# Layer norm two blocks later, a halved merge, another bank for the sigmoid, halved copies, and expert 30 scattered in two float32r parts

## The chip, the cores and the metric

One Trainium2 chip, one core. The metric is the device time of one execution of the whole program in microseconds (us), from the first instruction to the last; the figure that stands for a kernel is the median of its runs.

## The reference, cut to what matters

A decoder block over 256 tokens of 1024 channels, all in float32. In front, an adaLN-modulated RMS norm gives h, and `p = h @ w_in` gives 8 sections of 1024 columns, of which two feed a convolution branch, four an HGRN2 recurrence, and two are gates:

```python
u = conv(a * sigmoid(b), dw) + dw_bias            # 31 taps along the sequence
y_conv = silu(layernorm(u, ln_g, ln_b)) @ w_conv_out
y_hg = hgrn2(q, f, i, g) @ w_hgrn_out
merged = sigmoid(gc) * y_conv + sigmoid(gh) * y_hg
x = x + ga1 * (merged @ w_out)
```

Behind it stands a mixture of 32 experts of which each token takes four. Per expert, with xb its tokens:

```python
u = xb @ w1[e] + b1[e]                             # 1024 -> 2048
gl, lin = minimum(u[:, :1024], 7), clip(u[:, 1024:], -7, 7)
y = (gl * sigmoid(1.702 * gl) * (lin + 1)) @ w2[e] + b2[e]
out[tokens] += y * weight
```

The block ends in a final RMS norm of `x + ga2 * out`.

## The kernel before, in words

**Front.** The weights of the dense products come in 44 blocks of 1 MB (32 of w_in, then four each of ho, co and wo: the two branch outputs and w_out). Each block is split into float32r parts, high and low, in two halves (`split_half`, L381 to L401): ScalarE casts the high part (L393), VectorE or GpSimd subtracts it to get the low part (L395). `SPLIT_DVE` and `SPLIT_HALF` name the blocks whose subtraction VectorE does. A block's product is 48 matmuls of 256 columns on TensorE (L409, three per pair of parts). The halves of block n + 1 are split in program order within the product of block n.

After each block of w_in the kernel steps lists of jobs by one piece: `norms` (the recurrence's output, L592 on), `mods` (adaLN sections, L343), `lns` (the layer norm of the convolution, `layer_norm`, L553 on) and `taps` (the convolution's 31 taps on VectorE, L460). At block `LN_FROM` = 23 all taps that are left are emitted, and then the layer norm is appended; its five pieces run after blocks 23 to 27. The first piece sums `cv`, the convolution's output, over channels on TensorE (`mup`, L255), so it needs the last tap. The second gives the mean (`mu`, L264 and L563). The third subtracts it on VectorE (L565), squares on ScalarE (L569) and sums on TensorE (`varp`, L571). The fourth takes the root (L229, L230) and scales (L579). The fifth is 16 ScalarE activations and four multiplications (L586 to L589). The result is read when it is split for the co products (L416).

**Merge.** After each of the four co blocks, `tm = ps * gate + gate` (L807, L808) is split into float32r parts: `hi` by a ScalarE copy (L810), `lo` by VectorE (L811). `mg[0]` holds blocks 0 and 1, `mg[1]` blocks 2 and 3. The wo products read channel tiles kt 0 to 3 from `mg[0]` and 4 to 7 from `mg[1]`, so kt 6 and 7 are block 3's two halves.

**Experts.** The loop runs over experts 0 to 31; the order of TensorE and of SP's DMA queue is written by hand, while the order of the other engines is set by the framework's scheduler up to the last expert's second layer, from where ScalarE and VectorE are by hand too. Weights come in tiles of 1 MB through 22 slots: eight of w1 and four of w2 per expert. A slot's next load is issued when the products that read it are done. `first_layer` (L1007) fills two PSUM banks, `up[0]` (u_gl) and `up[1]` (u_lin), 64 token rows twice, and then: `gl = min(up[0])` (L1026), sigmoid on ScalarE into `si`, which lies in `up[0]` (L1027), the clip of `up[1]` (L1028), and two more VectorE operations (L1029, L1030). `turn` transposes the result on TensorE into a bank `ta` (L1043), ScalarE copies it (L1045), and `second_layer` reads it (L1058). An odd expert also gathers the tokens of the next pair (`xg_ps`, L983) and turns the pair's one-hot round (`rows_back`, L996 on); gather and transposes stand between the two layers.

The second layer's result is scaled (L1068), and a pair is scattered into four accumulator banks `acc` during the next even expert (`scatter`, L1079). For the pairs up to 28 and 29 the one-hot is unweighted (a comparison with zero, L1002, in float32r) and the weight `by` (L1004) goes into two float32r parts of the result (L1071, L1072). For the last pair (`last`, set when expert 29 makes it) `rows_back` returns a weighted float32 one-hot and no `by`, and expert 30 is scattered alone, in float32, in two parts: one inside expert 31's first layer at kt 4, one after it. At the same kt 4 ScalarE copies `owtx` (L1290) and `ga2x` (L1292), which the last expert's end uses (L1360, L1364). The last expert works in halves (`pieces` = 2), and its second layer, L1377, ends with the residual, the norm and the stores.

An expert with more than 64 tokens runs a branch for the rest (`small_first`, `small_second`, L1091 to L1171). `out_of` empties a PSUM bank in two halves, one on ScalarE (L1110) and one on VectorE (L1111).

Of the kernel before, what the change touches and what calls it, by code (L numbers as in the profile page):

```python
# [17 lines left out]
P = 128  # L18
# [24 lines left out]
TAPS = (1, 0, 0, 0, 5, 4, 10, 6, 5, 5, 13, 6, 16, 14, 17, 11, 5, 8, 0, 6, 0, 0, 0, 0, 0, 3, 13, 9, 17, 15, 9, 5)  # L43
LN_FROM = 23
SPLIT_DVE = (3, 4, 6, 28, 29, 30, 31, 37, 38, 40, 42)
# [45 lines left out]
def block_kernel(ctx, tc, xT_d, x_d, prm_d, con_d, wada0_d, wada_d, bada_d, gfin_d, win_d, wco_d, who_d, wo_d,  # L91
# [620 lines left out]
    for n, b in enumerate(IN_ORDER):  # L712
# [57 lines left out]
        if n in MOD_AT:  # L770
            step(mods, 1)
        elif n > MOD_AT[0]:
            step(mods, MOD_EXTRA.get(n, 0))
        if n == LN_FROM:
            step(taps, 1000)
            lns.append(layer_norm())
# [23 lines left out]
    for b in range(4):  # L800
        ps = block_product(36 + b, yx, "co_ps", last=b == 3)
        if b == 2:
            split_half(40, 0)
        if b % 2 == 0:
            mg.append(split_slot(f"mg{b // 2}"))
        tm = temp("tm").rearrange("p (m t) -> p m t", m=2)
        nc.vector.tensor_tensor(out=tm, in0=ps, in1=gate(b, 0), op=ALU.mult)  # L807
        nc.vector.tensor_tensor(out=tm, in0=tm, in1=gate(b, 1), op=ALU.add)  # L808
        hi, lo = (mg[b // 2][:, j, b % 2 * 2:b % 2 * 2 + 2, :] for j in range(2))
        nc.scalar.copy(out=hi, in_=tm)  # L810
        nc.vector.tensor_tensor(out=lo, in0=tm, in1=hi.bitcast(F32), op=ALU.subtract)  # L811
        if b % 2 == 1:
            free()
        step(preps, 2)
# [176 lines left out]
    def rows_back(o, last=False):  # L991


        wt_ps = bank("wt_ps")[:, 0:T]
        for t in range(NT):
            nc.tensor.transpose(wt_ps[:, t * P:(t + 1) * P], o[:, 1, t, :], ident)  # L996
        if last:
            owt = back()
            nc.scalar.copy(out=owt, in_=wt_ps)
            return owt, None  # L1000
        owt = back(dt=F32R)
        nc.vector.tensor_scalar(out=owt, in0=wt_ps, scalar1=0.0, scalar2=None, op0=ALU.not_equal)  # L1002
        by = med.tile([P, 1], F32, tag="by", bufs=2, name="by")
        nc.vector.tensor_reduce(out=by, in_=wt_ps, axis=mybir.AxisListType.X, op=ALU.add)  # L1004
        return owt, by

    def first_layer(xg, i, w1s, hot, pieces=1):  # L1007
# [14 lines left out]
        li = temp("li")  # L1022
        si = up[0]
        for c in range(0, 512, 512 // pieces):
            c = slice(c, c + 512 // pieces)
            nc.vector.tensor_scalar(out=gl[:, c], in0=up[0][:, c], scalar1=LIMIT, scalar2=None, op0=ALU.min)  # L1026
            nc.scalar.activation(si[:, c], gl[:, c], AF.Sigmoid, scale=ALPHA)  # L1027
            nc.vector.tensor_scalar(out=li[:, c], in0=up[1][:, c], scalar1=LIMIT, scalar2=-LIMIT, op0=ALU.min, op1=ALU.max)  # L1028
            nc.vector.scalar_tensor_tensor(out=li[:, c], in0=li[:, c], scalar=1.0, in1=gl[:, c], op0=ALU.add, op1=ALU.mult)  # L1029
            nc.vector.tensor_tensor(out=li[:, c], in0=li[:, c], in1=si[:, c], op=ALU.mult)  # L1030
# [7 lines left out]
    def turn(li, at_, pieces=1, piece=0):  # L1038
        ta = bank("ta")
        n = 4 // pieces  # L1040
        for j in range(piece * n, (piece + 1) * n):
            c = pick_columns(li, j) if pieces == 1 else li[:, j * P:(j + 1) * P]
            nc.tensor.transpose(ta[:, j * P:(j + 1) * P], c, ident)  # L1043
        c = slice(piece * n * P, (piece + 1) * n * P)
        nc.scalar.copy(out=at_[:, c], in_=ta[:, c])  # L1045

# [44 lines left out]
    def small_first(o, places, weights, hot, w1s, at_, owt, a, b, ps, u):  # L1091
# [20 lines left out]

        out_of(ps)
        for t in range(NT):
# [154 lines left out]
    for e in range(E_RUN):  # L1269
# [4 lines left out]
        if e == E_RUN - 1:  # L1274
            gfin = fetch(("gfin",))
            nc.gpsimd.partition_broadcast(gfin[:, 1, :], gfin[0:1, 0, :])  # L1276
            gfin = [gfin[:, 1, g * 512:(g + 1) * 512] for g in range(2)]
            owtx = back()
            ga2x = [temp("ga2x") for _ in range(2)]
        if i == 1 and e + 1 < E_RUN:  # L1280
# [4 lines left out]
        def w1s(kt):  # L1285
            if e == E_RUN - 1 and kt == 4:

                scatter(*before, slice(0, CAP), ts=(0,))
                for h in range(2):
                    nc.scalar.copy(out=owtx[h * 64:(h + 1) * 64, :], in_=owt[64:128, :])  # L1290
                    for g in range(2):
                        nc.scalar.copy(out=ga2x[g][h * 64:(h + 1) * 64, :], in_=ga2[g * 64:(g + 1) * 64, :])  # L1292
            if inline and kt == KT // 2:
# [8 lines left out]
        if i == 0 and e > 0:  # L1302
            scatter(*before, slice(0, 2 * CAP))
            owt, by = nxt
        if inline:
# [6 lines left out]
        if e == 0:  # L1312
            start_acc(1)
            gather(o, xg, 1)
            owt, by = rows_back(o)
        if i == 1 and e + 1 < E_RUN:
# [12 lines left out]
        if inline:  # L1329
            skip_ahead(f"second{e}" if e != RELOAD_AFTER else "reload")  # L1330
        if e == E_RUN - 1:
            break
        yp = second_layer(at_, lambda k2: keep(w2h, ("w2", e, k2)) if inline else take(("w2", e, k2)), hot)
# [149 lines left out]
```

## Time and profile before

| | us |
|---|---|
| runs | 1322.40, 1324.36, 1326.33 |
| median | 1324.36 |
| the profiled execution's own time | 1321.67 |
| its span, first to last instruction | 1319.9 |
| TensorE busy in the span | 1219.9 (92%) |
| VectorE, ScalarE, GpSimd busy | 545.2, 286.5, 163.4 |
| read from HBM | 477.11 MB, 362 GB/s over the span |

A difference between two kernels is read against the median; the profiled execution is 2.69 us shorter than that, and its span leaves out 1.77 us around it. In the page's strips of 40 slices one slice is 33 us: the front ends in the twelfth, and the experts take the rest. TensorE's busy time counts matmuls whose ends are modelled, so where the weights stream at the DMA's full rate a busy TensorE need not be the bound.

### The profile page before, as it was taken

How to read it: one execution, taken by the hardware profiler on the slowest of the kernel's cores; microseconds unless marked ns; L12 is line 12 of the kernel's file. 1: busy time of each engine (PE TensorE's matmuls, PEld its weight loads, DVE VectorE, ACT ScalarE, POOL GpSimd, SP SyncE). 2: the span in 40 equal slices, each digit the busy share in tenths (PEclk: the TensorE clock that was granted, in tenths of full speed). 3: DMA queues.
4: the chain of work that ended last, by engine and by line, in shares of the span. 5: the costliest groups of instructions: out<-in, count | busy, mean ns of one | idle time of the engine just before them, and what ended most of it. 6: DMA issues, size and time to landing. Idle time of an engine off the chain costs nothing. (4 is left out here: it accounts for less than half of the span.)

```text
span 1319.9 us, 19185 instructions
## 1 busy us (share of the span) xinstructions
PE 1219.9 (92%) x7829; PEld 669.9 (51%) x7829; DVE 545.2 (41%) x1121; ACT 286.5 (22%) x449; POOL 163.4 (12%) x78
## 2 busy tenths in 40 slices
PE   7999998999899999999999889988888898999997
PEld 6899788779864343443434333332323243434432
DVE  4498996545644242332323223232222232323322
ACT  4445444664720010001000000100000000100112
POOL 3258665222300000000000000000000000000000
PEclk9999989999999999999999899999999998999999
DMA  9993335656689999999999999999999999999995
GB/s 381 410 406 130 130 129 198 235 205 236 255 324 410 421 410 419 420 420 419 421 420 421 421 419 421 420 420 420 421 420 418 420 421 419 421 403 420 420 419 202
DMA packets 71399, 480.02 MB, mean 364 GB/s; under 512 B 7521, under 2 KB 8801, under 8 KB 15970
## 3 DMA queue, kind: packets, MB, share of 16 engines
q1 hardware_dynamic: 70834, 477.47, 88.5%
q8 instruction: 91, 1.49, 0.5%
q10 hardware_dynamic: 432, 0.72, 0.2%
q14 instruction: 42, 0.34, 0.1%
HBM read 477.11 MB, written 1.05 MB: 362 GB/s over the span
## 5 line engine op out<-in xcount | busy, mean ns | idle before, releaser
L1019 PE MATMUL u_gl<-w_w,xg 128*64 128x512 f32 x1024 | 270.1, 599 | 23.6 <-DMA w_w<-in_w_dram 23.6
L1019 PE MATMUL u_lin<-w_w,xg 128*64 128x512 f32 x1024 | 266.8, 592 | 0.0
L1058 PE MATMUL yp<-w_w,li 128*64 128x512 f32 x992 | 227.2, 606 | 19.1 <-ACT li L1045 10.5
L1019 PEld LDWEIGHTS u_gl<-w_w,xg 128*64 128x64 f32 x1024 | 75.9, 137 | 165.1 <-issue 88.8
L1026 DVE TENSOR_SCALAR gl<-u_gl 128x512 f32<-128x512 f32 (+1 forms) x33 | 22.3, 675 | 329.1 <-PE u_gl L1019 321.2
L1019 PEld LDWEIGHTS u_lin<-w_w,xg 128*64 128x64 f32 x1024 | 80.6, 137 | 140.0 <-issue 139.9
L1058 PEld LDWEIGHTS yp<-w_w,li 128*64 128x64 f32 x992 | 71.7, 139 | 156.5 <-issue 133.9
L409 PEld LDWEIGHTS p_ps<-h,ws 128*128 128x128 f32 x1152 | 141.4, 194 | 12.1 <-issue 5.9
L409 PE MATMUL p_ps<-h,ws 128*128 128x256 f32 x1152 | 146.2, 287 | 0.0
L1068 DVE TENSOR_TENSOR yg<-yp,ga 64x512 f32<-64x512 f32 x60 | 41.3, 689 | 225.6 <-PE yp L1058 225.0
L395 POOL TENSOR_TENSOR ws<-w_in,ws 128x1024 fp32r<-128x1024 f32 x45 | 113.1, 2527 | 87.2 <-ACT ws L393 77.8
L1276 POOL PARTITION_BROADCAST w_gfin<-w_gfin x1 | 1.3, 1305 | 898.6 <-DMA w_w<-in_w_dram 898.6
L1027 ACT ACTIVATE u_gl<-gl 128x512 f32<-128x512 f32 (+1 forms) x33 | 19.4, 589 | 427.2 <-DVE gl L1026 427.2
L460 DVE SCALAR_TENSOR_TENSOR cv<-u,pre,cv 128x229 f32<-128x229 f32 (+28 forms) x240 | 95.2, 456 | 8.6 <-ACT cv L457 7.9
L983 PE MATMUL xg_ps<-o,w_x 128*128 128x128 f32 (+1 forms) x544 | 65.4, 278 | 13.5 <-DVE li L1028 10.3
L1071 ACT ACTIVATE ys0h<-yg,by 64x512 fp32r<-64x512 f32 x30 | 21.6, 720 | 254.0 <-DVE yg L1068 254.0
L393 ACT CAST ws<-w_in 128x1024 fp32r<-128x1024 f32 x64 | 65.7, 1047 | 46.7 <-PE p_ps L409 17.6
L983 PEld LDWEIGHTS xg_ps<-o,w_x 128*128 128x128 f32 x544 | 62.2, 192 | 26.6 <-DVE li L1028 21.7
L987 DVE TENSOR_SCALAR xg<-xg_ps,g,sh 128x128 f32<-128x128 f32 (+1 forms) x136 | 45.3, 396 | 16.5 <-PE xg_ps L983 11.6
L1045 ACT COPY li<-ta 128x512 f32<-128x512 f32 (+1 forms) x33 | 18.9, 573 | 114.6 <-PE ta L1043 109.2
L395 DVE TENSOR_TENSOR ws<-w_in,ws 128x1024 fp32r<-128x1024 f32 x19 | 27.1, 1439 | 11.2 <-ACT ws L393 11.2
L409 PE MATMUL wo_ps<-ws,mg 128*128 128x256 f32 x192 | 26.0, 295 | 2.7 <-DVE mg L811 2.0
(292 smaller groups left out, 1158.1 us busy)
## 6 DMA issues: line engine op xcount, KB each, us to landing
w_w<-in_w_dram SPq DMA_DIRECT2D x380, 1024.0 KB, 19.9
w_in<-in_win_dram SPq DMA_DIRECT2D x32, 1024.0 KB, 11.0
w_ada<-in_wada_dram SPq DMA_DIRECT2D x24, 1024.0 KB, 16.3
w_ho<-in_who_dram SPq DMA_DIRECT2D x4, 1024.0 KB, 8.2
w_co<-in_wco_dram SPq DMA_DIRECT2D x4, 1024.0 KB, 8.4
w_wo<-in_wo_dram SPq DMA_DIRECT2D x4, 1024.0 KB, 9.6
w_w<-in_w_dram SPq DMA_DIRECT2D x8, 512.0 KB, 15.2
xT<-in_xT_dram SPq DMA_DIRECT2D x1, 1024.0 KB, 6.9
```

The source lines that it names most:

```text
L393: nc.scalar.copy(out=to[:, 0], in_=w[:, ks, :])
L395: (nc.vector if dve else nc.gpsimd).tensor_tensor(out=to[:, 1], in0=w[:, ks, :], in1=to[:, 0].bitcast(F32), op=ALU.subtract)
L409: nc.tensor.matmul(out, lhsT=lt, rhs=rh, start=first and kt == 0 and i == 0, stop=kt == KT - 1 and i == 2, skip_group_check=not first)
L460: nc.vector.scalar_tensor_tensor(out=cv[:, ct, s:], in0=u[i][:, m, :T - s], scalar=tap, in1=cv[:, ct, s:], op0=ALU.mult, op1=ALU.add)
L983: nc.tensor.matmul(ps[:, i, cs], lhsT=x2[:, t, kt * P:(kt + 1) * P], rhs=o[:, 0, t, cs], start=t == 0, stop=t == NT - 1)
L987: nc.vector.tensor_scalar(out=xg[h][:, i, cs], in0=ps[:, i, cs], scalar1=g2[:, kt:kt + 1], scalar2=sh2[:, kt:kt + 1], op0=ALU.mult, op1=AL ...
L1019: nc.tensor.matmul(up[nb][g * 64:(g + 1) * 64, :], lhsT=xg[kt // 4][:, kt % 4, i * CAP:(i + 1) * CAP], rhs=w[:, c:c + 512], start=False, s ...
L1026: nc.vector.tensor_scalar(out=gl[:, c], in0=up[0][:, c], scalar1=LIMIT, scalar2=None, op0=ALU.min)
L1027: nc.scalar.activation(si[:, c], gl[:, c], AF.Sigmoid, scale=ALPHA)
L1058: nc.tensor.matmul(yp[g * 64:(g + 1) * 64, :], lhsT=aT[:, kt % 4, kt // 4, :], rhs=w[:, kk, g * 512:(g + 1) * 512], start=False, stop=kt = ...
L1068: nc.vector.tensor_tensor(out=y[rows, :], in0=yp[gs, :], in1=ga2[gs, :], op=ALU.mult)
L1071: nc.scalar.activation(hi[rows, :], y[rows, :], AF.Copy, scale=by[rows, :])
```

## The change

Six edits. The layer norm is appended at block 25, while the taps are still emitted at block 23. Block 3's merge is done in two halves, with `hi` copied by VectorE. The sigmoid goes to `up[1]`, and the clip is issued ahead of it. `turn` copies two transposes at a time. The overflow branch empties its first bank in one ScalarE copy. The last pair gets the unweighted one-hot and `by` as the pairs ahead of it do, with the weighted one kept as `own` for `owtx`; `ga2x` is made after expert 31's first `turn`.

```diff
-LN_FROM = 23
+TAPS_END = 23
+LN_FROM = 25
...
+        if n == TAPS_END:
+            step(taps, 1000)
         if n == LN_FROM:
-            step(taps, 1000)
             lns.append(layer_norm())
...
-        nc.vector.tensor_tensor(out=tm, in0=ps, in1=gate(b, 0), op=ALU.mult)
-        nc.vector.tensor_tensor(out=tm, in0=tm, in1=gate(b, 1), op=ALU.add)
         hi, lo = (mg[b // 2][:, j, b % 2 * 2:b % 2 * 2 + 2, :] for j in range(2))
-        nc.scalar.copy(out=hi, in_=tm)
-        nc.vector.tensor_tensor(out=lo, in0=tm, in1=hi.bitcast(F32), op=ALU.subtract)
+        for m in (slice(0, 1), slice(1, 2)) if b == 3 else (slice(0, 2),):
+            nc.vector.tensor_tensor(out=tm[:, m], in0=ps[:, m], in1=gate(b, 0)[:, m], op=ALU.mult)
+            nc.vector.tensor_tensor(out=tm[:, m], in0=tm[:, m], in1=gate(b, 1)[:, m], op=ALU.add)
+            if b == 3:
+                nc.vector.tensor_copy(hi[:, m], tm[:, m])
+            else:
+                nc.scalar.copy(out=hi[:, m], in_=tm[:, m])
+            nc.vector.tensor_tensor(out=lo[:, m], in0=tm[:, m], in1=hi[:, m].bitcast(F32), op=ALU.subtract)
...
+        own = None
         if last:
-            owt = back()
-            nc.scalar.copy(out=owt, in_=wt_ps)
-            return owt, None
+            own = back("own")
+            nc.scalar.copy(out=own, in_=wt_ps)
         owt = back(dt=F32R)
...
-        return owt, by
+        return owt, by, own
...
-        si = up[0]
+        si = up[1]
...
+            nc.vector.tensor_scalar(out=li[:, c], in0=up[1][:, c], ..., op0=ALU.min, op1=ALU.max)
             nc.scalar.activation(si[:, c], gl[:, c], AF.Sigmoid, scale=ALPHA)
-            nc.vector.tensor_scalar(out=li[:, c], in0=up[1][:, c], ..., op0=ALU.min, op1=ALU.max)
...
-        c = slice(piece * n * P, (piece + 1) * n * P)
-        nc.scalar.copy(out=at_[:, c], in_=ta[:, c])
+        for j in range(piece * n, (piece + 1) * n, 2):
+            c = slice(j * P, (j + 2) * P)
+            nc.scalar.copy(out=at_[:, c], in_=ta[:, c])
...
-        out_of(ps)
+        nc.scalar.copy(out=a, in_=ps)
...
             owtx = back()
-            ga2x = [temp("ga2x") for _ in range(2)]
...
-                    nc.scalar.copy(out=owtx[h * 64:(h + 1) * 64, :], in_=owt[64:128, :])
-                    for g in range(2):
-                        nc.scalar.copy(out=ga2x[g][h * 64:(h + 1) * 64, :], in_=ga2[g * 64:(g + 1) * 64, :])
+                    nc.scalar.copy(out=owtx[h * 64:(h + 1) * 64, :], in_=own[64:128, :])
...
         if e == E_RUN - 1:
+            ga2x = [temp("ga2x") for _ in range(2)]
+            for g in range(2):
+                for h in range(2):
+                    nc.scalar.copy(out=ga2x[g][h * 64:(h + 1) * 64, :], in_=ga2[g * 64:(g + 1) * 64, :])
             break
```

## Rows read from the trace of the kernel before

**Rows 1.** The page's strip of DMA rates in 40 slices of 33 us, GB/s.

```profile
GB/s 381 410 406 130 130 129 198 235 205 236 255 324 410 421 410 419 420 420 419 421 420 421 421 419 421 420 420 420 421 420 418 420 421 419 421 403 420 420 419 202
```

**Rows 2.** The view of windows at the start of the experts: the stretch, its length, busy us of TensorE, its weight loads, VectorE, ScalarE and GpSimd with their counts, then TensorE's granted clock, the DMA's busy share and GB/s.

```profile
382.00:388.00 6.00, 6.00 (x41) 3.44 (x42) 2.63 (x11) 0.00 (x0) 0.00 (x0) 1.00 0.53 190
```

**Rows 3.** The view of waits, 900 to 1000 us (the middle of the experts): the engine and line that waited and for whom, us in total, times, the longest.

```profile
PE u_gl L1019 <- DMA w_w<-in_w_dram: 9.7, 17, 0.9
```

**Rows 4.** The timeline of TensorE, 1070 to 1135 us (experts 24 and 25): start in us, us, engine, line, operation, out<-in and count, and in brackets the idle time of the engine before it with its releaser.

```profile
1089.07 1.07 PE L1058 MATMUL yp<-w_w,li 128*64 128x512 f32 x2 [0.34 <-ACT li L1045]
1093.72 9.36 PE L1058 MATMUL yp<-w_w,li 128*64 128x512 f32 x30 [3.58 <-issue]
...
1120.04 1.10 PE L1120 MATMUL arm_ps<-arm 128*128 128x64 f32 x8 [1.24 <-DVE arm L1111]
```

**Rows 5.** The view of waits, 1130 to 1283 us (from expert 25's overflow branch to the start of expert 31), columns as in rows 3.

```profile
PE yp L1058 <- ACT li L1045: 2.0, 6, 0.3
...
PE xg_ps L983 <- DVE li L1028: 1.6, 2, 0.8
```

**Rows 6.** The view of windows at the end, columns as in rows 2.

```profile
1290.00:1300.00 10.00, 10.00 (x39) 3.26 (x39) 1.61 (x4) 0.39 (x1) 0.00 (x0) 1.00 0.92 348
1300.00:1305.00 5.00, 4.41 (x18) 1.29 (x18) 1.60 (x4) 1.61 (x4) 0.00 (x0) 1.00 0.46 176
```

**Rows 7.** The timeline of all engines, 1288 to 1320 us (expert 31 and the end), columns as in rows 4.

```profile
1289.72 1.98 PE L1079 MATMUL acc<-ys,owt 64*128 64x512 f32 x4
...
1300.08 0.42 DVE L1030 TENSOR_TENSOR li<-li,u_gl 128x256 f32<-128x256 f32 x1
...
1300.89 0.44 PE L1043 MATMUL ta<-con,li 128*128 128x128 f32 x2
...
1304.13 0.37 ACT L1045 COPY li<-ta 128x256 f32<-128x256 f32 x1 [2.39 <-PE ta L1043]
...
1304.56 5.37 PE L1377 MATMUL yp<-w_w,li 128*64 128x512 f32 x24
```

**Rows 8.** The timeline of TensorE, 195 to 345 us, columns as in rows 4.

```profile
220.75 0.64 PE L255 MATMUL mup<-cv,pre 128*32 128x256 f32 x2 [3.65 <-DVE cv L460]
221.32 7.46 PE L409 MATMUL p_ps<-h,ws 128*128 128x256 f32 x48
...
230.17 6.10 PE L409 MATMUL p_ps<-h,ws 128*128 128x256 f32 x48
```

**Rows 9.** The view of windows behind that stall, columns as in rows 2.

```profile
221.00:223.00 2.00, 2.00 (x10) 1.69 (x9) 0.35 (x1) 0.37 (x1) 0.00 (x0) 0.55 0.93 389
```

**Rows 10.** The timeline of all engines, 225 to 300 us (the layer norm and the blocks beside it), columns as in rows 4.

```profile
239.16 2.19 ACT L569 ACTIVATE csq<-cv 128x512 f32<-128x512 f32 x4
...
239.85 2.09 PE L571 MATMUL varp<-csq,pre 128*32 128x256 f32 x12 [0.44 <-ACT csq L569]
...
251.07 1.28 ACT L229 ACT_TABLE_LOAD   x1
...
262.15 1.09 ACT L586 ACTIVATE sigy<-cv,pre 128x256 f32<-128x256 f32 x2
...
269.05 1.08 ACT L587 ACTIVATE cv<-cv,pre 128x256 f32<-128x256 f32 x2
...
273.65 1.05 ACT L393 CAST ws<-w_in 128x1024 fp32r<-128x1024 f32 x1 [0.56 <-PE p_ps L409]
```

**Rows 11.** The timeline of all engines, 282 to 380 us, around the last merge, columns as in rows 4.

```profile
343.58 4.48 PE L409 MATMUL wo_ps<-ws,mg 128*128 128x256 f32 x36
...
345.15 0.68 DVE L807 TENSOR_TENSOR tm<-co_ps,gates 128x512 f32<-128x512 f32 x1
...
347.18 1.05 ACT L393 CAST ws<-w_wo 128x1024 fp32r<-128x1024 f32 x1
...
348.31 5.14 POOL L395 TENSOR_TENSOR ws<-w_wo,ws 128x1024 fp32r<-128x1024 f32 x2 [9.94 <-ACT ws L393]
...
348.78 2.43 DVE L811 TENSOR_TENSOR mg<-tm,mg 128x512 fp32r<-128x512 f32 x1 [2.21 <-ACT mg L810]
...
348.80 0.50 PE L409 MATMUL wo_ps<-ws,mg 128*128 128x256 f32 x2 [0.74 <-ACT mg L810]
...
351.26 8.56 PE L409 MATMUL wo_ps<-ws,mg 128*128 128x256 f32 x58 [1.96 <-DVE mg L811]
353.80 0.42 DVE L845 TENSOR_TENSOR tmo<-wo_ps,ga 128x256 f32<-128x256 f32 x1 [2.59 <-PE wo_ps L409]
```

**Rows 12.** The view of windows behind that wait, columns as in rows 2.

```profile
351.30:353.00 1.70, 1.70 (x8) 1.70 (x9) 0.00 (x0) 0.00 (x0) 1.70 (x1) 0.50 1.04 439
```

**Rows 13.** The timeline of all engines, 1240 to 1285 us (experts 29 and 30), columns as in rows 4.

```profile
1244.45 3.84 PE L983 MATMUL xg_ps<-o,w_x 128*128 128x128 f32 x32 [0.78 <-DVE li L1028]
...
1249.02 0.59 ACT L1045 COPY li<-ta 128x512 f32<-128x512 f32 x1
...
1249.66 7.09 PE L1058 MATMUL yp<-w_w,li 128*64 128x512 f32 x32 [0.34 <-ACT li L1045]
...
1271.19 0.50 PE L1079 MATMUL acc<-ys0h,owt 128*128 128x512 f32 x1
...
1273.66 0.72 PE L1043 MATMUL ta<-con,li 128*128 128x128 f32 x4 [0.33 <-DVEq L1308]
...
1275.03 2.50 ACT L1292 COPY ga2x<-ga 64x512 f32<-64x512 f32 x4
```

More of the change, by code (lines that the diff above doesn't have):

```diff
@@ L1026, in first_layer @@
             nc.vector.tensor_scalar(out=gl[:, c], in0=up[0][:, c], scalar1=LIMIT, scalar2=None, op0=ALU.min)
+            nc.vector.tensor_scalar(out=li[:, c], in0=up[1][:, c], scalar1=LIMIT, scalar2=-LIMIT, op0=ALU.min, op1=ALU.max)
             nc.scalar.activation(si[:, c], gl[:, c], AF.Sigmoid, scale=ALPHA)
-            nc.vector.tensor_scalar(out=li[:, c], in0=up[1][:, c], scalar1=LIMIT, scalar2=-LIMIT, op0=ALU.min, op1=ALU.max)
             nc.vector.scalar_tensor_tensor(out=li[:, c], in0=li[:, c], scalar=1.0, in1=gl[:, c], op0=ALU.add, op1=ALU.mult)
@@ L1303, in block_kernel @@
             scatter(*before, slice(0, 2 * CAP))
-            owt, by = nxt
+            owt, by, own = nxt
         if inline:
@@ L1314, in block_kernel @@
             gather(o, xg, 1)
-            owt, by = rows_back(o)
+            owt, by, own = rows_back(o)
         if i == 1 and e + 1 < E_RUN:
```

## The prediction, made blind

> **What bounds the kernel now.** I read the strips first, then the waits by stretch, then the timeline where a wait is long. The experts stream weights at 418 to 421 GB/s in 24 of the last 28 slices, while the front runs the DMA at about half of that [rows 1]. So the front is set by compute and the experts mostly by the stream. The stream starts when the front ends: from 382 to 388 us the DMA still idles half the time, because slots come free only as expert 0's products go through TensorE [rows 2]. What the front saves therefore moves the whole stream, one for one.
>
> The stream does not set the end, however. Between 900 and 1000 us TensorE waits for weights 17 times [rows 3]. At 1090 us expert 24 loses time on "issue", expert 25 runs the overflow branch [rows 4], and from then to expert 31 the waits of the matmuls are for other engines [rows 5]. The last weights land at about 1302.3 us (1300 plus 0.46 of 5 us [rows 6]), but TensorE is busy with the second layer until 1309.9 [rows 7]. TensorE is thus late by about 7 us, and its savings from expert 25 on count too. Between the two, a saving on TensorE only lengthens a wait for weights.
>
> How late it is bounds the last gain. Expert 31's w2 is 4 MB, 10 us at 420 GB/s, so its last w1 tile lands at about 1292.3. TensorE reads that tile at about 1297.0, 1.7 us (one tile's eight records) ahead of the second scatter, which ends at 1300.6 and takes 1.9 [rows 7]. This leaves 4.7 us to gain up to there.
>
> **1. The layer norm two blocks later.** The first sum over `cv` waits 3.65 us for the last taps with all of TensorE behind it, and the 48 matmuls behind it take 7.46 us where the next block's 48 take 6.10 [rows 8]. In that stretch the granted clock is 0.55, near the lower of the two levels, 1.2 GHz, where it had been 2.4 [rows 9]. The taps are still emitted at block 23. At block 25, two products of 6.1 us later, they are long done, so both losses go: 3.65 + 1.36 = 5.0 us. What is late next? Blocks 24 and 25 were split before the stall, so their products can follow at once. But ScalarE now has the norm's work in blocks 27 to 29, with the recurrence's output beside it and the casts of later blocks (the two of block 30 end at 274.7, behind the sigmoids, and wait for a slot [rows 10]). Now the squares make TensorE wait 0.44 us [rows 10]. There is no row for the new neighbours: the loss lies between nothing and the sigmoid piece, 262.15 to 270.1 or 8.0 us [rows 10]. I take 1.0, near the row of the present wait, since the casts can still be ordered ahead of a piece that nothing needs for several blocks. Net 4.0 us (-3.0 to 5.0).
>
> **2. The halved merge.** Now the wo product runs 36 matmuls to 348.06, then waits 0.74 us for ScalarE's `hi` and 1.96 for `lo`; the 58 matmuls behind take 8.56 us where 58/48 of 6.10 are 7.37, at a granted clock of 0.50 [rows 8, 11, 12]. That is 2.70 + 1.19 = 3.9 us. After the change block 3 takes eight VectorE operations of 128x256, 0.42 us each by the nearest row [rows 11]. The copy's own price shows nowhere; I use the same 0.42, which is what two-operand work of that size costs, and zero to 0.68 bounds it. Started at 345.15, the first half (kt 6) is ready at 346.8 and the second at 348.5; TensorE wants kt 6 at about 348.0 and kt 7 six matmuls, 0.75 us, later [rows 11]. The stall goes. Next in line is block 41, whose low parts GpSimd makes from 348.31 to 353.45 [rows 11]: its first half is ready at about 350.9, and TensorE would arrive at 349.6. I charge 0.9 of this. Net 3.0 us (0 to 3.9).
>
> VectorE's `lo` took 2.43 us against 0.68 for the multiplication of the same size at 345.15, while GpSimd worked [rows 11]. The Trainium skill, page "SBUF — State Buffer", section "Who interferes with whom", says that a VectorE operation with two SBUF inputs, or a copy in a two-port mode, and a GpSimd operation shut each other out for a whole instruction. By that rule this edit, which turns two operations of the kind (the addition and the subtraction) into six, could lose its gain; that case is rival B, and its price follows from the rows.
>
> **3. Experts 25 to 30.** With the sigmoid in `up[1]`, the first bank is free after the minimum, before TensorE is done with the second. The gather of an odd expert, which waits 0.78 us for the clip, need not [rows 5, 13]: 2 x 0.78 = 1.6 (experts 27 and 29; in 25 the branch stands between). The sigmoid now waits for the clip, 0.7 us more of delay; the gather of 3.84 us covers it in odd experts [rows 13], the scatter (1271.19 to 1273.33, eight records) nearly in even ones [rows 13]: at worst 0.2 each. The halved copy costs ScalarE 2 x 0.37 instead of 0.59 [rows 7, 13], but its first half ends before the bias matmuls do, so TensorE's 0.34 us per expert goes: six times, 2.0 [rows 5]. The single copy in the branch (0.59 on ScalarE) replaces a sequence that ended with VectorE's half, at a wait of 1.24 [rows 4]: 0.2. Sum 3.8 us (2.5 to 4.0). The same edits in earlier experts are hidden by the stream.
>
> **4. The end.** Each of the two float32 scatters takes four records, 1.91 us; the pairs' float32r ones take eight in 2.14 (1271.19 to 1273.33), so four take about 1.0 [rows 7, 13]. That gives 1.8 us, on TensorE's own path. Expert 30's two products gain ScalarE and VectorE work (0.7 us operations, half a dozen) that starts seven us ahead of the first scatter: free. What is late next is `li`: its first half ends at 1300.50, and the transposes start at 1300.9 [rows 7]. With the scatter 0.9 shorter they wait up to 0.5. Then `ga2x`: four copies, 2.50 us [rows 13], now stand in a gap of ScalarE of 2.39 [rows 7], ahead of the second `turn`'s copy, unless the scheduler puts some earlier. I charge 0.4 (0 to 1.2). Net 0.9 us (0 to 1.8).
>
> **Sum.** 4.0 + 3.0 + 3.8 + 0.9 = 11.7 us. Up to the last w1 tile parts 3 and half of 4 make 4.7, as much as the weights allow. Against the profiled execution's 1321.67 this gives 1310.0; that execution is 2.69 faster than the median of 1324.36, and against the median the forecast is **1312.7 us**.
>
> **Rivals.**
>
> A. *The norm's stall only moves.* ScalarE is in order; the squares or the casts then make TensorE wait about 4 us in blocks 27 to 31. For it: the casts already stand behind the sigmoids. Against it: two blocks of slack are left. 1312.7 + 4.0 = 1316.7.
>
> B. *GpSimd shuts VectorE out of the merge.* Two operations blocked at 2.43 - 0.68 = 1.75 each are 3.5 us, more than part 2. Against it: GpSimd starts at 348.31, when the chain is nearly done [rows 11]. 1315.7.
>
> C. *Expert 24's loss on "issue" goes or another comes.* It costs 3.58 us and then 9.36 - 7.09 x 30/32 = 2.7 at a slow clock, 6.3 in all [rows 4, 13], just ahead of the stretch where TensorE sets the end. Code of another length can shift such a wait: 1306.4 without it, 1319.0 with a second one behind it.
>
> D. *The front's gain stops at the stream.* Then only parts 3 and 4 are left, 1324.36 - 4.7 = 1319.7. Against it: the idle DMA of [rows 2].
>
> E. *Slower: the norm bunches up on ScalarE.* Squares 2.2, sigmoids 8.0 and two table loads of 1.28 [rows 10] in front of the casts of blocks 30 and 31 give 12.8 us, GpSimd's subtraction behind the cast 2.6 [rows 11], two slow stretches of 1.36: 18.1. Above 12.7 us of such waits (5.0 + 3.0 + 3.8 + 0.9) it is slower than before: 1324.36 + 18.1 - 12.7 = 1329.8. Against it: in the kernel before the same pieces beside the same products left TensorE waiting 0.44 us.
>
> F. *An edit does not do what it says*, as when the scheduler orders VectorE so that the merge's halves come out one behind the other: about 1315.7 too.
>
> **How the numbers follow.** Forecast 0.40, A 0.13, B 0.14, C faster 0.10 and slower 0.07, D 0.08, E 0.05, F 0.03. The range reaches from C's gain together with the upper bounds of the parts (5.0 + 3.9 + 4.0 + 1.8 = 14.7, or 1309.7 without C) up past D: 1304.5 to 1321. It leaves out E and the far ends. A measurement of this kernel tells about 0.3%, 4.0 us, from no change; so faster means below 1320.4. All cases but part of D and of C's slower side, and E, lie there: faster 0.84, the same 0.11, slower 0.05.
>
> **What would show it.** In the profile after: no wait of `mup` for the taps and no granted clock near 0.55 behind it; the wo product without waits for `mg`, or with one for GpSimd; the first expert's products some 7 us earlier; no 0.34 us ahead of the second layers and no 0.78 ahead of gathers; float32r scatters of 1.0 us in expert 31. The forecast is wrong if TensorE waits for ScalarE's casts in blocks 27 to 31, if the stream starts no earlier, or if TensorE waits for weights in expert 31.

## The result, and the profile after

The changed kernel took **1315.67 us** (median of 8 runs, 1313.03 to 1321.19), the kernel before 1325.27 beside it (8 runs); ratio 0.9939, interval 0.9924 to 0.9955, or 8.1 us less by the ratio (the two medians are 9.6 apart). The forecast was 1312.7 (1304.5 to 1321). The profiled execution took 1314.05 us with a span of 1312.4, so 7.6 less than that of before (7.5 by the spans). The differences below are read between these two.

**The front.** The page's strip of DMA rates after [rows 1], then the window at the start of the experts [rows 2] and two at the end [rows 6], columns as there:

```profile
GB/s 382 410 411 133 131 130 235 259 192 194 300 344 395 421 421 420 420 421 419 421 420 420 419 420 420 420 420 421 420 421 417 420 420 421 420 415 420 419 415 205
```

```profile
382.00:388.00 6.00, 6.00 (x32) 1.96 (x30) 0.00 (x0) 0.00 (x0) 0.00 (x0) 1.00 0.99 391
1290.00:1300.00 10.00, 8.75 (x38) 2.97 (x36) 3.90 (x9) 4.78 (x9) 0.00 (x0) 1.00 0.60 227
1294.00:1299.00 5.00, 4.64 (x21) 1.57 (x23) 0.35 (x2) 2.65 (x5) 0.00 (x0) 1.00 0.44 165
```

The stretch in which the DMA half idled is over by 382 us, and its last stretch (share 0.44) lies about 6 us earlier than that of before (0.46 [rows 6]); the landing of the last w1 tile, read further down, says 5.4. The first expert's weights meet TensorE at 377.24 instead of 384.49, 7.25 us earlier, where 7.0 were forecast:

```profile
384.49 1.03 PE L1019 MATMUL u_gl<-w_w,xg 128*64 128x512 f32 x4
```

```profile
377.24 1.03 PE L1026 MATMUL u_gl<-w_w,xg 128*64 128x512 f32 x4
```

But it is put together otherwise. TensorE before, at the starts of block 23, of block 30 and of the first `ho` product; then TensorE around the layer norm in the changed kernel, from the start of block 23, and ScalarE at the norm's end:

```profile
207.88 6.02 PE L409 MATMUL p_ps<-h,ws 128*128 128x256 f32 x48
...
277.64 6.31 PE L409 MATMUL p_ps<-h,ws 128*128 128x256 f32 x48
...
294.01 6.20 PE L409 MATMUL ho_ps<-o,ws 128*128 128x256 f32 x47
```

```profile
206.04 6.01 PE L410 MATMUL p_ps<-h,ws 128*128 128x256 f32 x48
...
214.01 6.00 PE L410 MATMUL p_ps<-h,ws 128*128 128x256 f32 x48
...
229.20 1.05 PE L256 MATMUL mup<-cv,pre 128*32 128x256 f32 x16
230.18 6.02 PE L410 MATMUL p_ps<-h,ws 128*128 128x256 f32 x48
...
268.04 6.31 PE L410 MATMUL p_ps<-h,ws 128*128 128x256 f32 x48
...
279.64 0.80 PE L410 MATMUL p_ps<-h,ws 128*128 128x256 f32 x2 [3.44 <-ACT ws L394]
280.90 7.90 PE L410 MATMUL p_ps<-h,ws 128*128 128x256 f32 x46 [0.46 <-DVE ws L396]
...
289.95 10.28 PE L410 MATMUL ho_ps<-o,ws 128*128 128x256 f32 x81
```

```profile
269.63 1.09 ACT L587 ACTIVATE sigy<-cv,pre 128x256 f32<-128x256 f32 x2 [2.12 <-DVE cv L580]
...
277.58 1.08 ACT L588 ACTIVATE cv<-cv,pre 128x256 f32<-128x256 f32 x2
278.56 1.98 ACT L394 CAST ws<-w_in 128x1024 fp32r<-128x1024 f32 x2
```

The stall at `mup` and the slow 48 matmuls behind it [rows 8] are gone. In their place block 31 waits 3.44 us for ScalarE's cast of its weights, which stands behind the whole sigmoid piece (269.63 to 278.56). Its 46 matmuls then take 7.90 us, at a granted clock of 0.50 to 0.56 from 280 to 286 us, where the 46 of another block take 5.78.

To leave out what came before, I count from the start of block 23's product (207.88 before, 206.04 after). Block 30's starts 69.8 us later before and 62.0 after, so 7.8 are gained: 3.65 and 1.36 of the stall and its slow clock, 0.44 of the squares, and 2.3 that I did not trace. From there to the first `ho` product it is 16.4 against 21.9, so 5.5 are lost. Net 2.2. The 1.8 us by which the changed kernel is ahead at block 23 I put down to chance: in the twelve profiles of the experiments, of either order, this start lies between 205.66 and 208.56.

Around the last merge [rows 11], in order of engine:

```profile
339.52 6.04 PE L410 MATMUL wo_ps<-ws,mg 128*128 128x256 f32 x49
346.68 5.90 PE L410 MATMUL wo_ps<-ws,mg 128*128 128x256 f32 x47 [1.12 <-POOL ws L396]
```

```profile
342.42 0.49 DVE L815 CAST mg<-tm 128x256 fp32r<-128x256 f32 x2
342.82 0.75 DVE L818 TENSOR_TENSOR mg<-tm,mg 128x256 fp32r<-128x256 f32 x2
345.48 0.42 DVE L852 TENSOR_TENSOR tmo<-wo_ps,ga 128x256 f32<-128x256 f32 x1 [1.90 <-PE wo_ps L410]
345.94 0.97 DVE L853 TENSOR_TENSOR w_x<-w_x,tmo 128x256 f32<-128x256 f32 x1
...
347.27 2.18 DVE L853 TENSOR_TENSOR w_x<-w_x,tmo 128x256 f32<-128x256 f32 x1
```

```profile
344.24 4.93 POOL L396 TENSOR_TENSOR ws<-w_wo,ws 128x1024 fp32r<-128x1024 f32 x2 [9.95 <-ACT ws L394]
```

No wait for `mg` is left, the next in line is GpSimd's block 41 as foreseen, 1.12 us for 0.9. The transposes behind it, before and after:

```profile
359.66 0.60 PE L828 MATMUL tp<-con,w_x 128*128 128x128 f32 x4
```

```profile
352.42 0.60 PE L835 MATMUL tp<-con,w_x 128*128 128x128 f32 x4
```

From the start of the product before the stall to these transposes, 343.58 to 359.66 became 339.52 to 352.42: 3.2 us less.

**The experts and the end.** The view of waits, 1130 to 1283 us [rows 5], and the chain that ended last, in order of time (start in us, us, what; before, see [rows 7]):

```profile
PE u_gl L1026 <- DMA w_w<-in_w_dram: 2.7, 5, 0.6
PE acc L1180 <- DVE arm L1176: 0.8, 1, 0.8
```

```profile
1269.79 19.47 DMA w_w<-in_w_dram
1289.26 0.04 issue
1289.31 1.08 PE u_gl L1026 x4
...
1292.22 0.62 ACT ga2x L1343
1292.85 0.47 ACT ga2x L1343
...
1294.23 1.94 PE yp L1389 x8
...
1297.00 5.37 PE yp L1389 x24
```

The 2.0 us for ScalarE's `li` and the 1.6 for the clip are gone, but TensorE now waits for weights where it did not before. The chain starts from the last w1 tile, which lands at 1289.26; TensorE starts on it at 1289.31. Before the second half can follow, two of the four `ga2x` copies stand on the path. From TensorE's first use of that tile to the end of the span it takes 23.1 us, as before (1296.83 to 1319.9). So the landing of the last w1 tile sets the time now, and what the edits save on TensorE ahead of it, beyond the slack there was, is waited away.

### The profile page after: what moved, and what is told of

Its sections match the earlier page's. It is cut to its first block, busy times and chain, and to the rows that moved or that the text cites. A ratio compares the mean times of both kernels' runs of the same rounds, so it can differ in the third digit from the quotient of the medians.

```text
span 1312.4 us, 19288 instructions
## 1 busy us (share of the span) xinstructions
PE 1217.0 (93%) x7829; PEld 668.0 (51%) x7829; DVE 544.7 (42%) x1129; ACT 289.4 (22%) x481; POOL 161.2 (12%) x78
## 5 line engine op out<-in xcount | busy, mean ns | idle before, releaser
L1068 PE MATMUL yp<-w_w,li 128*64 128x512 f32 x992 | 223.8, 603 | 8.0 <-issue 4.3
L1036 ACT ACTIVATE u_lin<-gl 128x512 f32<-128x512 f32 (+1 forms) x33 | 19.4, 589 | 429.6 <-DVE li L1035 429.6
L990 PE MATMUL xg_ps<-o,w_x 128*128 128x128 f32 (+1 forms) x544 | 69.5, 288 | 15.0 <-issue 12.4
L990 PEld LDWEIGHTS xg_ps<-o,w_x 128*128 128x128 f32 x544 | 66.5, 202 | 28.0 <-DVE gl L1034 13.9
L1055 ACT COPY li<-ta 128x256 f32<-128x256 f32 x64 | 20.8, 375 | 93.2 <-PE ta L1051 91.4
L1082 DVE SCALAR_TENSOR_TENSOR ys0l<-yg,by,ys0h 64x512 fp32r<-64x512 f32 x31 | 23.2, 748 | 14.3 <-ACT ys0h L1081 13.4
```

The lines of the kernel that those rows point to most:

```text
L990: nc.tensor.matmul(ps[:, i, cs], lhsT=x2[:, t, kt * P:(kt + 1) * P], rhs=o[:, 0, t, cs], start=t == 0, stop=t == NT - 1)
L1068: nc.tensor.matmul(yp[g * 64:(g + 1) * 64, :], lhsT=aT[:, kt % 4, kt // 4, :], rhs=w[:, kk, g * 512:(g + 1) * 512], start=False, stop=kt = ...
L1082: nc.vector.scalar_tensor_tensor(out=lo[rows, :], in0=y[rows, :], scalar=by[rows, :], in1=hi[rows, :].bitcast(F32), op0=ALU.mult, op1=ALU. ...
```

## Experiments

The theory T under test: the end goes by the stream of weights; the front's gain moves the stream; the norm's stall moved to block 31; parts 3 and 4 of the prediction are real on TensorE and mostly hidden by the stream. Ratios are to the kernel before, timed on the same chip.

**Each part alone.** Four kernels, each the kernel before with one part of the change.

```
a1  +TAPS_END = 23, LN_FROM = 25            a2  the loop over halves in the merge, b == 3
a3  si = up[1]; li before the sigmoid;      a4  own, owt, by = rows_back(...);
    turn's copy in halves; a<-ps in one         ga2x copied behind the first turn
```

> The kernel before with one edit: the layer norm's chain starts two blocks later. Theory T: the weights bound the stretch from 390 us to the end (412 to 421 GB/s in every 100 us there), so the end moves by what the first expert moves; the norm's stall of 3.65 us at the column sums is traded for one of 3.44 us and a slow clock at block 31, because the casts of block 31 stand behind the norm's sigmoids on ScalarE. Net gain of the front some 2 us: 1320.5 to 1324.5 us, most likely 1323. Rival P (the prediction's own term): 4.0 us, 1321. Rival S (the profile after shows a chance wait at block 31): 5 us, 1320. In the profile: TensorE's first p_ps product of block 31 waits 3 us or more for ScalarE's cast of the weights.

Measured: 1321.48 us, ratio 0.9976 (0.9964 to 0.9987), 3.2 us less. The time alone does not tell T's 2.2 from the prediction's 4.0 (the interval is 1.7 to 4.8 us); the trace does:

```profile
279.77 0.80 PE L410 MATMUL p_ps<-h,ws 128*128 128x256 f32 x2 [3.45 <-ACT ws L394]
```

The wait at block 31 comes with this edit alone, and from block 23's product to the first `ho` product it is 84.1 us, 2.0 less than before.

> The kernel before with the fourth merge block in two halves on VectorE, nothing else. Theory T: the 1.96 us wait and the slow clock behind it go, 3.2 us of the front, and the end moves as much since the weights that follow start earlier: 1320 to 1323 us. Rival: the front gains 3 us and the end nothing, because the first weights are not held back by this stage: 1325.

Measured: 1318.92, ratio 0.9957 (0.9940 to 0.9973), 5.7 us less, below the expected 1320 to 1323. All its five runs lie within 1.3 us. By their times, and by mean granted clocks of 0.983 to 0.987, they are runs in which a clock drop told of below did not come; against the runs of before near 1321.7 they are 2.8 less, so the end gets the front's 3.2 nearly whole. (In the two profiles the first expert starts 2.6 us earlier and the span is 2.4 shorter.)

> The kernel before with the experts' edits alone: sigmoid written into the other bank, the turn's copy in two halves, the branch's copy in one piece. The prediction gave these 3.8 us in experts 25 to 30 (1321.5). Theory T: they are worth under 1 us, since TensorE already waits for weights (23.6 us from 380 us to the end) and only waits longer for them: 1324 to 1326 us, with more and longer waits for the weights in its profile after 1000 us (12 us or more against 4 us in the profile of before) and the last w1 tile landing at the same time as before within 1 us. Rival: the slack of 4.7 us that the prediction read between the weights and TensorE at the end is there and the edits show 3 to 4 us.

Measured: 1323.38, ratio 0.9984 (0.9970 to 0.9997), 2.1 us less: between the two. The interval, 0.4 to 4.0 us, leaves room for either; T's "under 1" is unlikely. In this profile TensorE waits for weights 7.7 us from 1000 us on (3.8 before; 12 were expected), and for the very last w1 tile:

```profile
1300.19 1.08 PE L1019 MATMUL u_gl<-w_w,xg 128*64 128x512 f32 x4 [0.58 <-DMA w_w<-in_w_dram]
```

That tile lands 5.5 us later than in the profile of before, where T had it within 1: 2.6 us of this are there when the first expert starts, behind the clock drop told of below, and 3.5 by the experts' fortieth load; the rest I did not trace.

There is slack between the stream and TensorE at the end, but less than I had read. The last load that the DMA queue issues is held until the last w1 tile has landed: in the six profiles where TensorE waits for that tile (after, a3, b1, b2, c1 and c4) it starts within 0.05 us of TensorE's first use of it. In the kernel before, and then in the changed kernel (the view of a line: duration in ns, first and last start):

```profile
L126 SPq DMA_DIRECT2D w_w<-in_w_dram x1: 368/368/368, 1294.7 to 1294.7; - x1
```

```profile
L127 SPq DMA_DIRECT2D w_w<-in_w_dram x1: 368/368/368, 1289.3 to 1289.3; - x1
```

So the tile lands at 1294.7 in the kernel before, 5.4 us later than in the changed one. TensorE starts on it 2.2 us after that:

```profile
1296.83 1.03 PE L1019 MATMUL u_gl<-w_w,xg 128*64 128x512 f32 x4
```

The 2.1 us of a3 are what this slack lets through.

> The kernel before with the end's edits alone: the last pair but one scattered unweighted in two float32r parts, the gate's copies made behind the first turn. The prediction gave 0.9 us (1324.4). Theory T: four scatters get 0.85 us shorter each, two of them (1.7 us) ahead of the last w1 tiles, where TensorE then waits for weights instead; the other two count, but the gate's copies stand ahead of the second sigmoid's piece on ScalarE and cost 1.0 us: 1324 to 1326 us, no change that can be measured. Rival: 1.8 us are kept, 1323.5.

Measured: 1325.32, ratio 0.9999 (0.9986 to 1.0012): no change that can be measured, as T has it; but the interval, 1.9 us less to 1.6 more, shuts out neither the prediction's 0.9 nor the rival. With 2.8 for a2 the four add up to 8.2 us, each uncertain by 1.5 to 2, and the change as a whole gave 8.1.

**The norm's sigmoids in pieces.** In the changed kernel the loop's four turns are given out one a block:

```
             ys = cv[:, 2 * g:2 * g + 2, :]
             nc.vector.tensor_tensor(out=ys, in0=ys, in1=sy, op=ALU.mult)
-        yield
+            yield
```

> The changed kernel, with the norm's last step (16 activations, 9 us on ScalarE) given out in four pieces, one a block, instead of at once. Theory T: the casts of block 31 are then no longer behind it, the 3.44 us wait and some 2 us of slow clock at block 31 go, the first expert starts 4 to 6 us earlier and the end follows: 1309.5 to 1312 us. Rival: the pieces come into the output products' own casts and the gain is under 1.5 us: 1314 to 1316. Rival Q: the front gains 5 us but the end less than 2, because the weights do not start earlier.

Measured: 1310.14 us (1309.62 to 1311.87), ratio 0.9894 (0.9874 to 0.9913), 14.0 us less than before. Block 31 now:

```profile
276.56 0.50 PE L410 MATMUL p_ps<-h,ws 128*128 128x256 f32 x2
276.99 1.05 PE L344 MATMUL mod<-w_ada,pre 128*32 128x512 f32 x2
277.97 5.77 PE L410 MATMUL p_ps<-h,ws 128*128 128x256 f32 x46
```

No wait, and a granted clock of 1.00. From block 23's product to the first `ho` product it is 79.5 us, where the changed kernel takes 83.9: 4.4 of the 5.5 lost at block 31 come back. The first expert's weights meet TensorE at 374.12, 3.1 us earlier than in the changed kernel (block 23 had started 1.3 later by chance), the last w1 tile lands at 1286.03, 3.3 earlier, and the span is 3.3 shorter. Between these two kernels a microsecond of front is a microsecond of end; between before and after 7.25 us of front became 5.4 at the last w1 tile.

**The gate's copies later.** Moved behind the second turn's copy, in the changed kernel (b2) and together with the pieces (c1):

```
     if n == 0:
         turn(li, at_, 2, 1)
         start_y(1)
+        for gg in range(2): ... nc.scalar.copy(out=ga2x[gg][...], in_=ga2[...])
```

> The changed kernel, with the four copies of the gate made behind the second turn's copy on ScalarE instead of behind the first. Theory T: the wait of 0.97 us for the turn's copy at the second half of the last expert's first layer goes; the copies then stand ahead of the last products' scaling with 3 us to spare: 0.5 to 1.2 us less, 1314.5 to 1315.2. Rival: the copies come too late for the first scaling and the end is later by up to 1 us: 1316.5.

> The changed kernel with both edits: the norm's sigmoids in four pieces, and the gate's copies behind the second turn. Theory T: the pieces keep what they gave (block 31's wait of 3.44 us and its slow clock; 1310.1 us alone), the later copies take another 0.5 us off the tail behind the last weights, where nothing covers it: 1309 to 1310 us, at least 12 us under the kernel before. Rival: nothing beyond the pieces, or the copies in the way of the last scaling, 1310 to 1311.

Measured: b2 1315.28, ratio 0.9927 (0.9906 to 0.9947), beside 0.9939 for the changed kernel; c1 1311.39, ratio 0.9893 (0.9877 to 0.9909), beside 0.9894 for the pieces alone. Both lie above what T had (1314.5 to 1315.2, and 1309 to 1310), and c1 is nearer to its rival. The wait for the turn's copy is shorter, where T had it gone:

```profile
1297.20 1.94 PE L1386 MATMUL yp<-w_w,li 128*64 128x512 f32 x8 [0.46 <-ACT li L1055]
```

It was 0.97. From TensorE's first use of the last w1 tile to the end of the span it is 22.5 us in both profiles, for 23.1 in the changed kernel's and in b1's. The times cannot show half a microsecond, so what it is worth there stays open. The best version is the one with the pieces, at 1.1% under the kernel before.

**The stream out of the way.** Half of the first-layer weights of experts 23 and 24 are not loaded; TensorE's work stays as it is.

```
+CUT = (23, 24)
...
+            if e in CUT:
+                w1_src = [((slice(None), slice(0, FF)), w1_d[e, kt * P:(kt + 1) * P, 0:FF])]
...
-                    c = nb * FF + g * 512
+                    c = (0 if half else nb * FF) + g * 512
```

> The kernel before, but the first-layer weights of experts 23 and 24 are loaded only in half (their first 1024 columns stand for both halves), so 8 MB fewer, some 20 us of the stream, and TensorE's work is unchanged. Leaves out: half of those weights. Theory T: TensorE does not wait for weights from expert 24 on, the end is set by TensorE: the waits from 1000 us on (about 4 us) go, 1318 to 1322 us. It is the reference for the next kernel.

> The changed kernel with the same cut: half of the first-layer weights of experts 23 and 24 are not loaded. Theory T: with the stream out of the way the experts' and the end's edits count: 10 to 12 us less than the kernel before with the same cut (7 of the front, 3 to 4 of the experts, 0 to 1 of the end), 1307 to 1311 us, and no wait for weights in the last 200 us. Rival: the edits save nothing in themselves: 6 to 8 us less than the kernel before with the cut, as without it.

Measured: b3 1315.92 us, ratio 0.9947 (0.9928 to 0.9966); b4 1304.36, ratio 0.9848 (0.9828 to 0.9868). Their medians are 11.6 us apart, where the same two kernels with all weights are 9.6 apart; by the ratios it is 13.1 and 8.1, each uncertain by 2 to 3.6. So the times lean to T and do not settle it. The traces are plainer, with one execution of each: from the first expert's weights to the end of the span it is 935.4 us before and 935.2 after, so with all weights the edits behind the front give nothing beyond it, and 930.4 in b3 and 924.3 in b4, 6.1 less. Neither of the two waits for weights from 1000 us on. With weights at hand the change is thus worth about what the prediction's sum, 11.7, had it worth, though its parts are not those of the sum. (Both came out below what T had; from expert 23's start to 25's b3 takes 59.7 us, 65.5 before, and I had counted only the waits.)

> The kernel before with the experts' edits alone and with half of the first-layer weights of experts 23 and 24 not loaded (left out: half of those weights). To be read against the kernel before with the same cut (1315.9 us), where TensorE never waits for weights from 1000 us on. Theory T: with the stream out of the way the prediction's term is right in itself: 3.8 us, 1312 us (1311 to 1313.5), where the same edits gave 2.1 us without the cut. Rival: the term was too large in itself, and 2 us or less come: 1314 to 1316 us.

> The kernel before with the end's edits alone and the same cut of the weights of experts 23 and 24 (left out: half of them), against the kernel before with the cut (1315.9 us). Theory T: the scatter's 1.7 us count where no weight is waited for, less 0.5 to 0.9 us that the gate's copies put ahead of the second piece and the turn's copy: 0.8 to 1.2 us less, 1315. Rival: nothing or a loss, 1316 to 1316.5.

Measured: c2 1312.48, ratio 0.9908 (0.9891 to 0.9926), against b3's 0.9947 (0.9928 to 0.9966); c3 1316.41, ratio 0.9930 (0.9911 to 0.9949). These ran on another chip than b3, so by ratio they are 5.2 and 2.2 us under it, each uncertain by some 3.5; c3's median reads like the rival, but half of its runs, with mean granted clocks of 0.980 to 0.982 for 0.986, are 3 us longer or more than the others, as with the clock drop told of below. The traces are sharper. The start of experts 25 and 31 on TensorE, in b3 and then in c2:

```profile
1099.08 0.41 PE L1016 MATMUL u_gl<-b,hots 96*64 96x512 bf16 x2
...
1277.96 0.41 PE L1016 MATMUL u_gl<-b,hots 96*64 96x512 bf16 x2 [0.16 <-PEq L1346]
```

```profile
1094.90 0.41 PE L1016 MATMUL u_gl<-b,hots 96*64 96x512 bf16 x2 [0.16 <-PEq L1347]
...
1269.53 0.41 PE L1016 MATMUL u_gl<-b,hots 96*64 96x512 bf16 x2 [0.16 <-PEq L1347]
```

Experts 25 to 30 take 178.9 us in b3 and 174.6 in c2: 4.25 us for the prediction's 3.8. Of these expert 25 gives 1.9, the odd experts 27 and 29 0.87 each and the even ones 0.2 each. With all weights loaded the changed kernel shows 2.0 of this (1103.23 to 1282.30 before, 1094.49 to 1271.55 after). From expert 31's start to the end of the span it is 37.5 us in b3 and 36.6 in c3: 0.95 for the prediction's 0.9.

**The clock in the routing.** The runs of one kernel lie in two groups: of the kernel before, some near 1321.7 us and more near 1325.5. In 6 of the 14 profiles TensorE's granted clock falls to 0.5, the lower of its two levels (1.2 GHz), shortly before the first expert. These are a1, a3, b2, b4, c1 and c3, each in the upper half of its kernel's runs and four of them the very longest. The kernel a1, columns as in rows 2:

```profile
376.00:378.00 2.00, 1.69 (x15) 1.44 (x15) 2.00 (x15) 1.23 (x1) 0.00 (x0) 1.00 0.99 414
378.00:380.00 2.00, 2.00 (x14) 2.00 (x13) 1.96 (x9) 0.00 (x0) 0.00 (x0) 0.63 1.04 438
380.00:382.00 2.00, 2.00 (x11) 2.00 (x10) 0.00 (x1) 0.00 (x0) 0.00 (x0) 0.50 0.43 180
382.00:384.00 2.00, 2.00 (x10) 0.81 (x11) 1.18 (x5) 0.00 (x0) 0.00 (x0) 0.50 0.02 4
384.00:386.00 2.00, 2.00 (x10) 0.59 (x8) 0.00 (x0) 0.00 (x0) 0.00 (x0) 0.66 0.00 0
```

TensorE has gaps up to 378 us, then the clock falls while it is busy; expert 0 gives its slots back later, and the DMA stands still for 4 us. The kernel before with some of these gaps filled:

```
+    def keep_busy(n):
+        for _ in range(n):
+            nc.tensor.matmul(pcb[:, 256:384], lhsT=tri, rhs=tri, start=True, stop=True)
...
+    keep_busy(5)
...
         nc.tensor.matmul(pc[:, t, :], lhsT=tri, rhs=sel[:, t, :], start=t == 0, stop=True)
+        keep_busy(4 - t)
```

> The kernel before with some 12 short matmuls that nobody reads put into TensorE's gaps in the routing (between the residual and the first gather). Theory C: the kernel's times fall into two groups, near 1321.7 and near 1325.5 us, by whether TensorE's granted clock falls to 0.5 in the routing, 376 to 386 us, which makes the first expert's start 2.5 us later and lets the stream of weights pause longer; with the gaps filled the clock stays at 1.0 and all runs lie near 1321.7 to 1322.5 us (the fill itself costs 0 to 0.7 us). Rival: the groups have another cause, and the times stay in two groups with a median of 1324.5 to 1325.5 us; or the clock falls all the same.

Measured: 1321.60 us (12 runs, 1319.70 to 1323.35), ratio 0.9980 (0.9968 to 0.9991), 2.6 us less. One group, where the kernel before, beside it, has eleven runs from 1324.0 to 1327.1 and five from 1320.6 to 1322.5. The mean granted clock of each run goes the same way: 0.983 to 0.989 in all twelve, 0.978 to 0.982 in nine of the eleven long runs of the kernel before, and 0.982 to 0.986 in its five short ones. Theory C holds, though only one execution's trace shows the clock staying up there. With T it also says why medians of five or eight runs of the same kernel stray by 2 us.

## Why the prediction was right or wrong

**What bounds the kernel: half right.** That the front moves the stream is shown, nearly one for one in a2 and b1. "The stream does not set the end" fell: in the changed kernel it does, and in the kernel before it was nearer than I had it. The step that failed is "the last weights land at about 1302.3 us (1300 plus 0.46 of 5 us)". It takes the share for 2.3 us at the full rate, but the stretch began at 227 GB/s, the rate falls further, and the last packet of weights ends at 1304.6. The kernel before, columns as in [rows 6]:

```profile
1303.00:1304.00 1.00, 1.00 (x6) 0.20 (x2) 0.00 (x0) 0.00 (x0) 0.00 (x0) 1.00 0.40 152
1304.00:1305.00 1.00, 0.87 (x4) 0.30 (x5) 0.00 (x0) 0.85 (x2) 0.00 (x0) 1.00 0.13 49
```

The 10 us from the last w1 tile to that end were right by luck. They were "4 MB, 10 us at 420 GB/s"; in fact 2.7 MB are left when the tile lands (2.4 to 2.5 in the profiles where TensorE waits for it), since part of w2 has come in ahead of it, and they take 9.95 us at the lower rates. So the tile landed at 1294.7 and not at 1292.3, and the slack was 2.2 us, not 4.7.

**1. The norm: wrong on what is late next.** The stall and its slow clock went, and 7.8 us were gained up to block 30, more than the 5.0. Then block 31 lost 5.5 where I had taken 1.0 "since the casts can still be ordered ahead of a piece that nothing needs for several blocks". They are not: ScalarE ran the piece in one go, with the casts behind. The bound (8.0) held this, the choice didn't. Rival A came true: the waits at block 31 are 3.9 us, where it had about 4. The net is still 2.2 and not nothing, since more was gained ahead of it. b1 shows that the order of the pieces was most of it: 4.4 of the 5.5 come back.

**2. The merge: right**, 3.2 us for 3.0, and the next wait was the one named. Rival B did not come, for the reason given: VectorE had ended at 343.57 when GpSimd began at 344.24. Where VectorE did meet GpSimd, in the residual behind it, the addition with both inputs in SBUF took 0.97 and 2.18 us beside 0.42 for the multiplication of the same size that reads PSUM; before, with GpSimd done at 353.45, the same two additions took 0.42 each (354.26 and 355.06). By the Trainium skill's page "SBUF — State Buffer", section "Who interferes with whom", such an operation and GpSimd's shut each other out; these rows agree.

**3. Experts 25 to 30: near as work, wrong as time.** 4.25 us with the weights at hand, but not from the rows named: expert 25, with the overflow branch, gave 1.9 where 0.54 were counted, and the other five 2.4 for 3.3. As time it is 2.1 alone in the kernel before, about the slack, and in the changed kernel parts 3 and 4 share that slack.

**4. The end: right as work** (0.95 for 0.9), nothing as time: half of it lies ahead of the last w1 tiles, and the rest went to the `ga2x` copies on the path, the 0 to 1.2 us that were foreseen.

**Sum.** In the two profiles the last w1 tile lands 5.4 us earlier and the slack of 2.2 is used up: 7.6 us, all that was gained. The 5.4 are 2.2 and 3.2 of parts 1 and 2 and the 1.8 of chance ahead of block 23, less 1.9 that the stream loses on its way: load by load its lead is 7.2 to 8.3 us over the experts' first eighty loads, about 6 from the hundredth on and 5.4 at the last, and I did not trace why. The number came within 3 us and the sign was right, with two terms that failed for another reason than chance: the norm's 1.8, and 2.5 us of parts 3 and 4 behind the stream. The time is nearer to rival A's 1316.7 than to the forecast; that it meets the 1315.7 of B and F is an accident. Of the three signs by which the forecast was to be called wrong two came: TensorE waits for ScalarE's casts at block 31, and for weights in expert 31. (The range's lower end is also a slip: C's gain below 1309.7 is 1303.4, not 1304.5.)

**Rivals C, D, E, F.** The "issue" loss in expert 24 is gone in the changed kernel's profile, but one of 4.7 us came in expert 23, and from 23's start to 25's it is 64.2 us for 65.5; TensorE waits for weights there in both, so it decides nothing. The shift goes with the experts' edits: the seven profiles that have them (after, a3, b1, b2, b4, c1 and c2) all lose 4.5 to 4.9 us in expert 23's gather and nothing in expert 24's second layer. With weights at hand the same stretch is 59.7 us in b3 and 58.9 and 58.7 in b4 and c2, so the shift is worth about 1 us and not 6.3. D and F did not come; E's bunching came, at a third of its price.

## What to carry to other kernels

When a stall is moved, look for the work that each in-order engine will have between its new place and the next thing that waits: a long piece that nothing needs soon should be given out in small parts, so that urgent work never stands behind all of it. Where a stream runs at its full rate, ask of every saving whether it lies ahead of the stream's start or behind its end; in between, whatever goes beyond the slack turns into a wait. The slack between a stream and an engine is read from when the tile lands, and not from a mean share of a window or from bytes over rate.

## What the runs showed that was not expected

- The granted clock at the start of the experts falls in some executions and not in others of the same kernel, with gaps that look alike (TensorE busy 1.69 of 2 us just ahead of the fall in a1, 1.38 and 1.53 in the kernel before, where it held). Twelve short matmuls, 1.2 us together, made the kernel 2.6 us faster. The Trainium skill's page "TensorE: Matmul & The Clock Gate", section "Part 1: The HAM clock gate (the "warmup" mystery)", says that the number of matmuls at the low clock at a kernel's start differs from run to run of one kernel. The two groups here are of that kind, but the fall comes in the middle of the kernel, of which that passage does not speak.
- With the weights at hand expert 25 gained 1.9 us, of which the forecast had 0.54; which of its rows this is was not looked for.
- A float32 128x256 copy with rounding on VectorE took 0.49 us for two in a row, where two subtractions of the same size took 0.75; I had taken the same price for both.
